# Values and inverse products of each recurrent group tied to a counted number of other blocks' products; the visits of the state chain joined, on two banks

## The chip, the cores and the metric

The kernel runs on one core of one Trainium2 chip. The metric is the device time of one execution in microseconds (us), from the first to the last instruction and what little lies around them. Engines are named as in the profile: PE is the matmul engine (PEld its weight loads), DVE the vector engine, ACT the scalar engine, POOL the third elementwise engine, SP the engine from whose queue all DMAs are issued.

## The reference

One layer of a hybrid decoder on 1024 tokens of 1024 channels: three branches on the same normalised input, merged by gates, then a ConvFFN. Cut to what matters here:

```python
h = rms_norm(x, norm_mix_pre)
z = h @ w_in                                   # one input projection for all branches
z_pool, z_q, z_rwkv, z_gate = split(z)
y_pool = pool_branch(z_pool) @ w_proj_pool     # causal means over windows 2, 4, 8, 16
y_mem = mem_attention(z_q, mem_n) @ w_proj_mem # 4 heads into 256 memory tokens
r, k, v, dw, da, dg = split(zr)                # zr: z_rwkv mixed with its token shift
# recurrent branch, 16 heads of 64, for every token t:
sa = state @ a_t
state = state * w_t + sa b_t^T + v_t k_t^T
y_t = state @ r_t
# then a norm per head, + bonus: sum(r * k * r_k) * v, times a gate g
merged = g0 * y_pool + g1 * (y_rwkv @ w_proj_rwkv) + g2 * y_mem
x = x + rms_norm(merged @ w_o)
f = (gelu(u_gate) * u_val) @ w_ffn_down        # u: causal conv of rms_norm(x) @ w_ffn_up
x = x + rms_norm(f)
```

## The kernel before

**Products in three parts.** Activations lie transposed (channels on partitions, tokens along the row). A large product is made of three passes on values split into a high and a low part: `mm3` (L158) issues high x high (L161), high weights x low activations (L162) and low weights x high activations (L163). The input projection is cut into 58 blocks of 128 output channels. A block (`in_block`, L249) loads eight 128x128 weight pieces, two per DMA (`load_w`, L139: raw on SP's queue, high part on POOL or ACT, low part on POOL or DVE), and makes two halves of 512 tokens, each of eight steps; a step is the three products of one weight piece. So a block has 16 steps or 48 products. `hh` and `hl` hold the split input.

**Groups.** The 16 recurrent heads are done in four groups of two head pairs (`rwkv_group`, L376). A group has these stages:

- the vector stage (L390 to L446): decay and rate from their small projections, head sums (`phd`), scans, scaled copies `AR` and `BK` for each head pair, and the block of r (L421, in_block). At the end of each pair's part stands the bonus: a product of ones `pbo` (L442) that must stand behind the scaling of r (L439), its product with v on DVE (L443), ACT, and a store to `d_bv`, which is read back only at the group's end (L599).
- the values (`pv`, L458 and L459): v centred, into `HV`.
- the scores (`ps`, L479 and L486): products within chunks of 64 tokens, masked on DVE into `RB`, `NT` and `AR`; then BK scaled (L491) and transposed (`pt`, L496).
- the inverse: 32x32 triangles of both pairs inverted on DVE by substitution (L513 to L518), transposed (L519, L520), then completed by small products `pz` (L534) and `pw` (L541). All `pz` products stand behind L520.
- the state chain (L549 to L590): 16 rounds, one per chunk. In a round PE makes `pr`, DVE copies it to `Rs`, PE makes `pu`, DVE and ACT copy it into `HV`, PE makes `ph` (the new state) and `py` (the output, partly L564, partly L586), and DVE adds `ph` into the next state. `pr`, `pu` and `ph` use one bank (`psc`), one after another.
- the four blocks of k and v of the next group (`group_kv`, L354), then the head norm of this group's output (L595 to L613).

**What sets the order.** The framework lays down the order on each engine when the program is built. It takes the program's order as priority and places an instruction as soon as its own estimates say that its inputs are there; what is ready and stands later in the program goes into the gaps. Tiles of one tag take their buffers in program order. `later` (L199) adds an order between two instructions without a wait. 24 of the 32 blocks of the pooling input, the queries and the gates (`fill`, L616) stand behind the four groups in the program and have weight buffers and banks of their own (class 1), so that they can be drawn into the gaps of the groups. The last eight stand in the pooling stage (two per pool group, L739).

**After the groups** come the memory's keys and values (L643), the attention (L679), the pooling stage (L718), the projections of the memory branch (L763) and of the pooling branch (L773) and the rest. The tiles `pm` of the memory projection lie where `hh` and `hl` were. `load_w` without a class alternates between class 0 and class 1.

## Time and profile before

| | |
|---|---|
| median of 3 runs | 2258.53 us (2258.16 to 2258.91) |
| the profiled execution | 2256.94 us, of which span 2255.2 us |
| mean granted PE clock | 0.982 of full speed |
| groups 0 to 3 | about 114 to 1035 us of the span |
| PE, DVE, ACT, POOL busy | 96%, 52%, 37%, 34% of the span |

Times of single instructions are us from the start of the span. Where an engine waited, the views name what released it last. "PE pz L534 <- DVE tb L519" reads: the product into pz issued in line 534 stood until DVE's instruction on tb in line 519 was done. A row of a table by stretches gives the stretch, its length, then for each engine the busy time and, in brackets, the number of instructions, then the granted PE clock, the share of time in which DMA engines were busy, and GB/s.

### The profile page before, as it was taken

To read this page: it belongs to the slowest core of one execution; us is meant where nothing else is said; L and a number is where in the kernel's file an instruction comes from. 1 tells how busy PE (TensorE), PEld (TensorE's weight loads), DVE (VectorE), ACT (ScalarE), POOL (GpSimd) and SP (SyncE) were. 2 spreads that over 40 slices of the span, in tenths; PEclk is the share of its full clock that TensorE was granted. 3 is DMA by queue.
4 is the path that set the end of the run, shared out by engine and by line. 5 is a ranking of instruction groups with operands and counts; after the bars stand their busy time and mean duration, and the time that the engine had idled before them with its cause. 6 is when DMAs were issued, how large, how long until landed. Compare 5 with 4: busy or idle time off the path is not lost.

```text
span 2255.2 us, 34230 instructions
## 1 busy us (share of the span) xinstructions
PE 2155.7 (96%) x12630; PEld 1649.1 (73%) x12630; DVE 1176.7 (52%) x2101; ACT 837.1 (37%) x1696; POOL 766.4 (34%) x1025
## 2 busy tenths in 40 slices
PE   7999899989998999899989999999999999999998
PEld 4767566766676667667877878777888888888887
DVE  6277539653965386634764442767403423334237
ACT  3342234223432252224634244545433413323143
POOL 6552116222521242212153355556422222323240
PEclk9999999999998999999999999999999999999999
DMA  4311112112111121114336343543211111111123
GB/s 138 126 54 50 38 60 68 57 39 67 66 55 41 54 92 44 57 56 142 98 117 201 130 145 100 163 153 94 76 50 45 50 50 42 54 40 57 38 75 136
DMA packets 147319, 181.46 MB, mean 80 GB/s; under 512 B 15824, under 2 KB 115792, under 8 KB 147152
## 3 DMA queue, kind: packets, MB, share of 16 engines
q1 hardware_dynamic: 147152, 179.28, 24.4%
q8 instruction: 100, 1.64, 0.3%
q14 instruction: 67, 0.55, 0.1%
HBM read 141.46 MB, written 37.75 MB: 79 GB/s over the span
## 4 chain that ended last, share of the span: by engine, by line
PE 73%; DVE 17%; DMA 3%; ACT 3%; issue 2%; POOL 2%; SPq 0%; POOLq 0%; ACTq 0%; DVEq 0%
PE psg L161 20%; PE psg L162 20%; PE psg L163 20%; DVE tb L518 2%; DVE tb L516 2%; PE ps L486 2%; PE ps L479 1%; POOL wlo L127 1%; PE pr L554 1%; PE pu L560 1%; ACT tHV L191 1%; DVE AR L425 1%; PE py L564 1%; PE py L586 1%; DMA wraw<-in_w_in 1%
## 5 line engine op out<-in xcount | busy, mean ns | idle before, releaser
L127 POOL TENSOR_TENSOR wlo<-wraw,whi 128x256 fp32r<-128x256 f32 (+1 forms) x696 | 578.3, 835 | 686.7 <-ACT whi L124 606.3
L161 PE MATMUL psg<-hh,whi 128*128 128x512 f32 x928 | 389.2, 420 | 0.9 <-ACT hh L117 0.7
L162 PE MATMUL psg<-hl,whi 128*128 128x512 f32 x928 | 386.6, 417 | 1.6 <-DVE hl L118 1.6
L126 POOL TENSOR_SCALAR whi<-wraw 128x256 fp32r<-128x256 f32 x240 | 151.3, 630 | 695.4 <-PE psg L162 671.9
L163 PE MATMUL psg<-hh,wlo 128*128 128x512 f32 x928 | 384.1, 414 | 0.2
L124 ACT CAST whi<-wraw 128x256 fp32r<-128x256 f32 (+1 forms) x488 | 191.8, 401 | 361.5 <-PE psg L162 274.2
L161 PE MATMUL psg<-h2h,whi 128*128 128x512 f32 x704 | 279.7, 397 | 4.4 <-DVE zc L826 4.4
L163 PE MATMUL psg<-h2h,wlo 128*128 128x512 f32 x704 | 278.7, 396 | 1.2 <-POOL wlo L127 1.2
L162 PE MATMUL psg<-h2l,whi 128*128 128x512 f32 x704 | 278.6, 396 | 0.0
L161 PEld LDWEIGHTS psg<-hh,whi 128*128 128x128 f32 x928 | 177.0, 191 | 47.0 <-issue 2.2
L163 PEld LDWEIGHTS psg<-hh,wlo 128*128 128x128 f32 x928 | 177.4, 191 | 43.2 <-issue 2.2
L162 PEld LDWEIGHTS psg<-hl,whi 128*128 128x128 f32 x928 | 177.0, 191 | 43.0 <-DVE hl L118 2.5
L161 PEld LDWEIGHTS psg<-h2h,whi 128*128 128x128 f32 x704 | 132.4, 188 | 37.3 <-ACT whi L124 5.0
L163 PEld LDWEIGHTS psg<-h2h,wlo 128*128 128x128 f32 x704 | 132.3, 188 | 34.2 <-POOL wlo L127 1.6
L162 PEld LDWEIGHTS psg<-h2l,whi 128*128 128x128 f32 x704 | 132.4, 188 | 32.7 <-issue 0.5
L823 DVE SCALAR_TENSOR_TENSOR uv<-psg,pv,uv 128x511 f32<-128x511 f32 x44 | 33.0, 749 | 156.7 <-ACT uv L822 156.7
L163 PE MATMUL psg<-fh,wlo 128*128 128x512 f32 x288 | 113.8, 395 | 0.0
L162 PE MATMUL psg<-fl,whi 128*128 128x512 f32 x288 | 113.8, 395 | 0.0
L161 PE MATMUL psg<-fh,whi 128*128 128x512 f32 x288 | 113.6, 395 | 0.0
L823 DVE SCALAR_TENSOR_TENSOR ug<-psg,pv,ug 128x511 f32<-128x511 f32 x44 | 32.9, 749 | 146.2 <-ACT ug L822 146.2
L989 DVE TENSOR_TENSOR acc<-acc,psg 128x512 f32<-128x512 f32 x48 | 33.0, 687 | 102.5 <-PE psg L163 102.5
L276 ACT ACTIVATE st<-psg,pv 128x512 f32<-128x512 f32 x48 | 33.1, 690 | 108.9 <-PE psg L163 99.1
(341 smaller groups left out, 3975.0 us busy)
## 6 DMA issues: line engine op xcount, KB each, us to landing
wraw<-in_w_in SPq DMA_DIRECT2D x240, 128.0 KB, 2.3
wraw<-in_w_fup SPq DMA_DIRECT2D x216, 128.0 KB, 2.3
d_zg<-st SPq DMA_DIRECT2D x48, 256.0 KB, 2.6
wraw<-in_w_fdn SPq DMA_DIRECT2D x80, 128.0 KB, 2.1
wraw<-in_w_prwkv SPq DMA_DIRECT2D x64, 128.0 KB, 2.3
wraw<-in_w_o SPq DMA_DIRECT2D x64, 128.0 KB, 2.3
xr<-in_xT SPq DMA_DIRECT2D x16, 256.0 KB, 5.4
d_g<-st SPq DMA_DIRECT2D x16, 256.0 KB, 2.0
```

The costliest lines, as they stand in the source:

```text
L124: A.copy(hi, src)
L126: G.tensor_scalar(hi, src, 1.0, 0.0, op0=ALU.mult, op1=ALU.add)
L127: (V if lo_on_dve[0] else G).tensor_tensor(lo, src, hi.bitcast(F32), op=ALU.subtract)
L161: first = PE.matmul(ps, wh, xh, start=start, stop=False)
L162: PE.matmul(ps, wh, xl, start=False, stop=False)
L163: last_mm[0] = PE.matmul(ps, wl, xh, start=False, stop=stop).ins
L276: A.activation(st, ps, AF.Identity, bias=bias)
L486: PE.matmul(ps[:, c], BK[i][up, c0 + c], AR[up, i, 1:3, t], start=True, stop=True)
L516: V.tensor_tensor(tm, X[:, s + 1:, s:s + 1].broadcast_to([P, n, m]), S[:, s:s + 1, 0:m].broadcast_to([P, n, m]), op=ALU.mult)
L518: V.tensor_tensor(S[:, s + 1:, 0:m], S[:, s + 1:, 0:m], tm, op=ALU.add)
L823: V.scalar_tensor_tensor(d[:, 1:], ps[:, :511], col("cw1", j), d[:, 1:], op0=ALU.mult, op1=ALU.add)
L989: V.tensor_tensor(accs[n][:, j], accs[n][:, j], ps, op=ALU.add)
```

## The change

Four things are changed.

1. The 24 blocks are no longer behind the groups in the program. `fill_to(n)` issues whole blocks until at least n steps of them stand in the program, and returns the last product of step n. In group g the first value product is ordered behind step 95 g + 28, and the first inverse product `pz` behind step 95 g + 95 (380 of 384 in the last group). The order of every `pz` behind L520 is dropped.
2. The bonus of both head pairs is made behind the scores of the first pair, and no longer ordered behind the scaling of r.
3. In the state chain `pr`, `pu` and `ph` take turns on two banks (`psc` and `psk`).
4. The chain's products form three visits per round: `pr` with the first part of `py`; `pu`; `ph` with the second part of `py`. Within a visit each product is ordered behind the one before, and the first behind the last copy or sum that it needs.

The eight blocks of the pooling stage stay the same ones.

```diff
@@ gemm
+            if log is not None:
+                log.append(last_mm[0])
@@ rwkv_group, vector stage
             V.scalar_tensor_tensor(t0_, r_, col("r_k", p), t4_, op0=ALU.mult, op1=ALU.mult)
-            rt = V.tensor_tensor(r_, r_, t3_, op=ALU.mult).ins
+            V.tensor_tensor(r_, r_, t3_, op=ALU.mult)
+            vs.append(t1_)
+
+        def bonus(i):
+
+            t0_ = kv[i][:, 0]
             for t0, _ in HALVES:
+                s = slice(t0, t0 + 512)
                 ps = pss.tile([P, 512], F32, name="pbo", tag="s")
-                later(PE.matmul(ps, bones, t0_[:, t0:t0 + 512], start=True, stop=True), rt)
-                V.tensor_tensor(t0_[:, t0:t0 + 512], t1_[:, t0:t0 + 512], ps, op=ALU.mult)
-            A.activation(t0_, t0_, AF.Identity, bias=col("ln_b", p))
-            SP.dma_start(d_bv[p], t0_)
-            vs.append(t1_)
+                PE.matmul(ps, bones, t0_[:, s], start=True, stop=True)
+                V.tensor_tensor(t0_[:, s], vs[i][:, s], ps, op=ALU.mult)
+            A.activation(t0_, t0_, AF.Identity, bias=col("ln_b", 2 * g + i))
+            SP.dma_start(d_bv[2 * g + i], t0_)
...
+        place = fill_to(95 * g + 28)
...
-                    PE.matmul(ps[64:128, c], vs[i][0:64, tsl], cent[0:64], start=True, stop=True)
+                    m = PE.matmul(ps[64:128, c], vs[i][0:64, tsl], cent[0:64], start=True, stop=True)
+                    if i == c0 == c == 0:
+                        later(m, place)
...
+            for b in range(2 if i == 0 else 0):
+                bonus(b)
...
-        behind = V.transpose(X.rearrange("p u t -> p t u"), S).ins
+        V.transpose(X.rearrange("p u t -> p t u"), S)
+        place = fill_to(95 * g + 95)
...
-                    later(m, behind)
+                    if u0 == u == 0:
+                        later(m, place)
@@ state chain
+        turn = [0]
+
+        def bank(name):
+            turn[0] ^= 1
+            return (psc if turn[0] else psk).tile([P, 2, C], F32, name=name, tag="c" if turn[0] else "k")
+
+        def visit(products, after):
+
+            for (out_, l, r), kw in products:
+                m = PE.matmul(out_, l, r, **kw)
+                if after is not None:
+                    later(m, after)
+                after = m.ins
+            return after
+
+        ready = None
         for c in range(NCH):
             t = slice(c * C, (c + 1) * C)
-            pr = psc.tile([P, 2, C], F32, name="pr", tag="c")
+            once = dict(start=True, stop=True)
+            pr = bank("pr")
+            py = pss.tile([P, 2, C], F32, name="py", tag="s")
+            ke, ko = (up, lo) if c == 0 else (slice(0, P), slice(0, P))
+            row = []
             for i in range(2):
-                ke, ko = (up, lo) if c == 0 else (slice(0, P), slice(0, P))
-                PE.matmul(pr[lo, i], AR[ke, i, 0, t], HV[ke, i, c, 0], start=True, stop=True)
-                PE.matmul(pr[up, i], AR[ko, i, 2, t], HV[ko, i, c, 1], start=True, stop=True)
+                row.append(((pr[up, i], AR[ko, i, 2, t], HV[ko, i, c, 1]), once))
+                row.append(((pr[lo, i], AR[ke, i, 0, t], HV[ke, i, c, 0]), once))
+            for i in range(2 if c else 0):
+                kw = dict(start=i == 0, stop=False)
+                row.append(((py[lo, i], HV[lo, i, c, 0], AR[lo, i, 1, t]), kw))
+                row.append(((py[up, i], HV[up, i, c, 1], AR[up, i, 1, t]), kw))
+            visit(row, ready)
             Rs = rw.tile([P, 2, C], F32, name="Rs", tag="Rs", bufs=1)
             V.tensor_copy(Rs, pr)
-            pu = psc.tile([P, 2, C], F32, name="pu", tag="c")
+            pu = bank("pu")
+            visit([((pu[q, i], NT[q, i, c], Rs[q, i]), once) for i in range(2) for q in (lo, up)], None)
+            V.tensor_copy(HV[lo, :, c, 0], pu[lo])
+            ready = A.copy(HV[up, :, c, 1], pu[up]).ins
+            row = []
+            if c + 1 < NCH:
+                ph = bank("ph")
+                for i in range(2):
+                    row.append(((ph[up, i], BKN[i][:, c, 64:128], HV[:, i, c, 1]), once))
+                    row.append(((ph[lo, i], BKN[i][:, c, 0:64], HV[:, i, c, 0]), once))
             for i in range(2):
...
+                kw = dict(start=c == 0 and i == 0, stop=i == 1)
+                row.append(((py[lo, i], HV[:, i, c, 0], RB[i][:, 0, c]), kw))
+                row.append(((py[up, i], HV[:, i, c, 1], RB[i][:, 1, c]), kw))
+            visit(row, ready)
             if c + 1 < NCH:
...
                 for q, e in ((lo, 0), (up, 1)):
                     if c == 0:
-                        V.tensor_copy(HV[q, :, 1, e], ph[q])
+                        ready = V.tensor_copy(HV[q, :, 1, e], ph[q]).ins
                     else:
-                        V.tensor_tensor(HV[q, :, c + 1, e], ph[q], Hd[q], op=ALU.add)
+                        ready = V.tensor_tensor(HV[q, :, c + 1, e], ph[q], Hd[q], op=ALU.add).ins
...
@@ trunk_kernel
+    filled = []
+
+    def fill_to(n):
+
+        while len(filled) < n:
+            j, ev = fill.pop(0)
+            in_block(j, ev, 1, filled)
+        return filled[n - 1]
+
...
-    for j, ev in fill[:24]:
-        in_block(j, ev, 1)
...
-            n = 16 + 2 * gi
-            for j, ev in gates[n:n + 2]:
+            for j, ev in fill[2 * gi:2 * gi + 2]:
                 in_block(j, ev, 1)
```

More of the change, by code (lines that the diff above doesn't have):

```diff
@@ L164, in mm3, with gemm @@
         return first
-    def gemm(ws, rhs, width=512, behind=None, ps=None):
+    def gemm(ws, rhs, width=512, behind=None, ps=None, log=None):
         if ps is None:
@@ L247, in hrhs, with in_block @@
         return lambda k: (hh[:, k, t0:t0 + 512], hl[:, k, t0:t0 + 512])
-    def in_block(j, evac, c=0):
+    def in_block(j, evac, c=0, log=None):
         ws = load_w(w_in[j], KC, c=c)
         for t0, _ in HALVES:
-            evac(t0, gemm(ws, hrhs(t0)))
+            evac(t0, gemm(ws, hrhs(t0), log=log))
     def shifted(m, dst):
@@ L556, in rwkv_group @@
             Rs = rw.tile([P, 2, C], F32, name="Rs", tag="Rs", bufs=1)
             V.tensor_copy(Rs, pr)
-            pu = psc.tile([P, 2, C], F32, name="pu", tag="c")
-            for i in range(2):
-                PE.matmul(pu[lo, i], NT[lo, i, c], Rs[lo, i], start=True, stop=True)
-                PE.matmul(pu[up, i], NT[up, i, c], Rs[up, i], start=True, stop=True)
-            py = pss.tile([P, 2, C], F32, name="py", tag="s")
-            for i in range(2 if c else 0):
-                PE.matmul(py[lo, i], HV[lo, i, c, 0], AR[lo, i, 1, t], start=i == 0, stop=False)
-                PE.matmul(py[up, i], HV[up, i, c, 1], AR[up, i, 1, t], start=i == 0, stop=False)
@@ L566, in rwkv_group @@
-            V.tensor_copy(HV[lo, :, c, 0], pu[lo])
-            A.copy(HV[up, :, c, 1], pu[up])
+            pu = bank("pu")
[8 more added lines that the diff above has]
+                    row.append(((ph[lo, i], BKN[i][:, c, 0:64], HV[:, i, c, 0]), once))
@@ L568, in rwkv_group @@
+            for i in range(2):
+                kw = dict(start=c == 0 and i == 0, stop=i == 1)
+                row.append(((py[lo, i], HV[:, i, c, 0], RB[i][:, 0, c]), kw))
+                row.append(((py[up, i], HV[:, i, c, 1], RB[i][:, 1, c]), kw))
+            visit(row, ready)
             if c + 1 < NCH:
-                ph = psc.tile([P, 2, C], F32, name="ph", tag="c")
-                for i in range(2):
-                    PE.matmul(ph[lo, i], BKN[i][:, c, 0:64], HV[:, i, c, 0], start=True, stop=True)
-                    PE.matmul(ph[up, i], BKN[i][:, c, 64:128], HV[:, i, c, 1], start=True, stop=True)
@@ L584, in rwkv_group @@
                         A.activation(Hd[:, i], Hn[:, i], AF.Identity, scale=Dc[:, i, c + 1:c + 2])
-            for i in range(2):
-                PE.matmul(py[lo, i], HV[:, i, c, 0], RB[i][:, 0, c], start=c == 0 and i == 0,
-                          stop=i == 1)
-                PE.matmul(py[up, i], HV[:, i, c, 1], RB[i][:, 1, c], start=c == 0 and i == 0,
-                          stop=i == 1)
             A.copy(AR[:, :, 1, t], py)
@@ L714, in trunk_kernel @@
     as_ctx.close()
-    gates = fill[8:]
     with tc.tile_pool(name="pt", bufs=1) as pt_:
```

## The prediction, made before the result was known

> **What bounds the kernel now.** I read the page first, then who waited for whom on the matmul engine within the four recurrent groups (110 to 1040 us), then the granted clock right behind the longest wait.
>
> ```profile
> span 2255.2 us, 34230 instructions
> PE 2155.7 (96%) x12630; PEld 1649.1 (73%) x12630; DVE 1176.7 (52%) x2101; ACT 837.1 (37%) x1696; POOL 766.4 (34%) x1025
> ...
> PE pz L534 <- DVE tb L519: 30.3, 4, 7.7
> PE pbo L442 <- DVE kv L438: 12.6, 8, 3.5
> ...
> PE phd L372 <- DVE kv L443: 1.1, 4, 0.4
> PE pv L458 <- DVE kv L443: 0.8, 3, 0.3
> ```
>
> PE is busy for 96% of the span: it is the bound, and only three things can shorten the kernel: less PE idle time, less PE time at a low clock, less PE time per product. The waits (total, times, longest) name two places. Once per group PE stands about 7.6 us before the first inverse product (pz, L534) until DVE has finished the inverse (L519), and twice per group it stands before the bonus product (pbo, L442). With the two small followers these are 30.3 + 12.6 + 1.1 + 0.8 = 44.8 us.
>
> The clock comes next. The columns are stretch, length, busy time (instructions) of PE, PEld, DVE, ACT and POOL, granted clock, DMA share and GB/s; then three products of the first stretch.
>
> ```profile
> 241.00:248.30 7.30, 7.30 (x77) 5.26 (x77) 4.00 (x6) 3.65 (x7) 2.20 (x4) 0.50 0.06 20
> 469.96:476.90 6.94, 6.94 (x77) 5.27 (x77) 5.55 (x10) 4.31 (x7) 1.90 (x3) 0.50 0.06 19
> 697.84:704.80 6.96, 6.96 (x77) 5.27 (x77) 4.53 (x8) 4.88 (x8) 0.00 (x0) 0.50 0.01 2
> 928.82:935.00 6.18, 6.18 (x76) 4.83 (x77) 3.98 (x6) 3.13 (x6) 0.00 (x0) 0.54 0.01 3
> 209.00:233.50 24.50, 24.50 (x106) 19.36 (x104) 22.44 (x50) 3.00 (x6) 10.76 (x18) 1.00 0.26 86
> ...
> 850.90:854.80 3.90, 3.88 (x68) 2.62 (x68) 2.59 (x3) 1.13 (x1) 0.23 (x1) 1.00 0.11 35
> ...
> 246.10 0.63 PE L161 MATMUL psg<-hh,whi 128*128 128x512 f32 x1
> 246.53 0.63 PE L162 MATMUL psg<-hl,whi 128*128 128x512 f32 x1
> ```
>
> Behind each of the four waits PE runs some 7 us at half clock: its wide products start 0.43 us apart (246.10 to 246.53), against 24.50 / 106 = 0.231 us in the dense stretch before. So each wait costs more than its own length.
>
> **The change, part by part.** I count in steps of three wide products, 0.69 us each. The rows are the products on hh (columns: stretch, length, busy time and count, clock, DMA share, GB/s); two of a step's three use hh, so steps are the count halved. The page's count of L161 gives 928 steps in all.
>
> ```profile
> L161 PE MATMUL psg<-hh,whi 128*128 128x512 f32 x928 | 389.2, 420 | 0.9 <-ACT hh L117 0.7
> ...
> 0.00:928.80 928.80, 505.44 (x1451) 0.97 0.20 66
> 114.00:163.30 49.30, 34.77 (x108) 1.00 0.14 46
> 163.30:240.90 77.60, 37.24 (x111) 0.98 0.17 58
> 928.80:1141.00 212.20, 99.41 (x252) 0.98 0.26 87
> 1141.00:1212.00 71.00, 50.56 (x153) 0.95 0.39 132
> ```
>
> *Values and inverse behind counted steps.* In group 0 now 54 steps lie before the values and 55.5 between them and the inverse. Afterwards it is the group's 32 steps of r plus 28, that is 60, and then 95 - 28 = 67: 6 and 11.5 more, 17.5 x 0.69 = 12.1 us of work that is due anyway. It goes where PE now stands 44.8 / 4 = 11.2 us. So both waits should close and the group's first two stages keep their length; the counts overshoot by about 1 us, which is work, not loss. **Term 1: -44.8 us.** What is then late at the inverse is the count itself, not DVE.
>
> *Half clock.* Without a 7 us gap the products behind it run at full clock. Half of 27.4 us (the four stretches) is the upper bound, 13.7. The lower bound is the eleven wide products in each stretch, at 0.43 - 0.23 = 0.20 us: 8.8. I take **term 2: -11 us**. [...]
>
> *Bonus moved* behind the first head pair's scores. Its DVE work stays:
>
> ```profile
> L443 DVE TENSOR_TENSOR kv<-kv,pbo 128x512 f32<-128x512 f32 x4 | 2.5, 674 | 0.0
> ```
>
> Four of 0.67 us leave the vector stage and enter the score stage, before the BK scaling and the inverse. Earlier start and later work cancel: 0. If the earlier start isn't had, 2.7 us per group, 10.8 in all, delay the inverse. The bonus stores go to SP's queue later, but are read back only at the group's end (L599), so nothing waits.
>
> *The chain's visits.* A visit is a run of small products between wide ones. Rows of one round, then the one place where two visits already touch:
>
> ```profile
> 264.88 0.27 PE L554 MATMUL pr<-HV,AR 128*64 128x64 f32 x1
> ...
> 265.26 0.50 PE L162 MATMUL psg<-hl,whi 128*128 128x512 f32 x1
> ...
> 267.43 0.27 PE L586 MATMUL py<-RB,HV 128*64 128x64 f32 x1
> ...
> 268.09 0.50 PE L162 MATMUL psg<-hl,whi 128*128 128x512 f32 x1
> ...
> 268.75 0.27 PE L564 MATMUL py<-AR,HV 64*64 64x64 f32 x1
> ...
> 269.15 0.50 PE L161 MATMUL psg<-hh,whi 128*128 128x512 f32 x1
> 269.58 0.27 PE L554 MATMUL pr<-HV,AR 128*64 128x64 f32 x1
> ...
> 278.84 0.27 PE L565 MATMUL py<-AR,HV 64*64 64x64 f32 x1
> ...
> 279.10 0.27 PE L554 MATMUL pr<-HV,AR 128*64 128x64 f32 x1
> ...
> 279.48 0.33 PE L565 MATMUL py<-AR,HV 64*64 64x64 f32 x2
> ```
>
> A round lasts 269.58 - 264.88 = 4.70 us and has four visits; the py visit (L564) is now put with pr (L554). Apart the two cost 0.40 (268.75 to 269.15) + 0.43 for the wide product between, less its own 0.23, + 0.38 (264.88 to 265.26) = 0.98 us. Touching they cost 0.40 + 0.38 = 0.78, since pr takes 0.38 behind py too (279.10 to 279.48). So 0.20 us each, 15 rounds x 4 groups: **term 3: -12.0 us**. Sixteen products of one form take only 0.66 (267.43 to 268.09); at that price it would be 0.32 x 60 = 19. [...]
>
> The second bank costs nothing: psk's bank is otherwise used from L646 on. It spares pr the wait for the Hn sum, which is no bound now. The new order chains py behind the last copy; I price that as a rival.
>
> *What is taken from later.* By 928.8 us 725.5 steps are done now. With the change 26 blocks x 16 + 380 = 796 are done at that place (the fourth inverse), and 132 are left. The stages up to 1141 now take 126 as fill, so about 6 remain for the pooling stage, which now has 76.5.
>
> ```profile
> 1141.00:1212.00 71.00, 65.42 (x262) 50.08 (x261) 41.50 (x55) 21.39 (x36) 40.71 (x45) 0.95 0.39 132
> ...
> 1141.35 0.33 SPq L723 DMA_DIRECT2D tz<-d_zp  x1
> ...
> 1154.30 0.38 SPq L723 DMA_DIRECT2D tz<-d_zp  x1
> ...
> 1170.65 1.33 SPq L723 DMA_DIRECT2D tz<-d_zp  x1
> ...
> 1186.90 0.33 SPq L723 DMA_DIRECT2D tz<-d_zp  x1
> ...
> 1209.32 0.42 SPq L768 DMA_DIRECT2D pm<-d_zg  x1
> ...
> L161 PE MATMUL psg<-oh,whi x64: 392/395/398, 1209.8 to 1254.7; 128*128 128x512 f32 x64
> ```
>
> That stage has a chain of its own, one load and one pass of DVE per pool group, 13 to 16 us each: 1141.35 to 1186.90, and one more of about 16, makes some 63 us however little PE does. Now PE has 262 x 0.232 = 61 us of products there, in 71: 10 lost. What can fill it is the memory projection (192 products, oh), which starts at 1209.8, when the last block on hh is done and its memory free (pm at 1209.32). With that done by about 1145 its first products can come forward; but it alternates two weight and bank classes, and the second class shares its banks with the pool products, so I let half through: 96. Work then is 18 + 24 (pool) + 96 = 138 x 0.232 = 32 us in 63: 31 lost, 21 more than now. **Term 4: +21 us.** Ends: none comes forward, +43; all, about 0.
>
> Sum on the profiled execution's own time: 2256.9 - 44.8 - 11 - 12 + 21 = 2210.1. The median of the runs is 1.6 us above that execution, so **2212 us**.
>
> **The rivals.**
> *Nothing fills the pool stage*: the projection stays behind the pool products. For: it starts after the last block now. Price: 96 x 0.232 = 22 us; 2234.
> *All of it fills*: both classes come forward, 22 us less; 2190. For: pm waits for the last hh block alone in the rows.
> *The closed-up visits wait.* Now L564 stands right behind DVE:
>
> ```profile
> 268.75 0.13 PEld L564 LDWEIGHTS py<-AR,HV 64*64 64x64 f32 x1 [0.36 <-DVE HV L577]
> ```
>
> If one wide product too few is laid into the two gaps behind the copies, each round waits up to 2 x 0.23, 64 rounds 29 us; 2241. Against: the four gaps of a round hold nine wide products, and three gaps with fewer copies between need fewer.
> *Slower: the counted products come on top of the waits.* Place: 6 steps before the values, 11.5 before the inverse. If they only delay the scores, the inverse starts later by as much and PE stands as before: +12.1 x 4 = 48.4, terms 1 and 2 gone. Then only the visits (12) and the shorter late stages are left: pooling and projection last 1255 - 1141 = 114 us now and 63 + 22 = 85 then, 29 less. 2258.5 + 48.4 - 12 - 29 = 2266. It decides from 41 of the 48 us on top. Against: the wait ends with DVE, and steps laid before it are used up while DVE works.
> *Nothing happens*, because the order hardly moves: 2258.
>
> **How the numbers follow.** Forecast 2212: 0.45. Pool stage empty, 2234: 0.20. Full, 2190: 0.14. Visits wait, 2241: 0.08. On top, 2266: 0.08. No effect: 0.05. Under 0.2% (4.5 us) this kernel can't be told from no change. Faster 0.87, same 0.05, slower 0.08. The range 2187 to 2240 takes the first three cases with the bounds of terms 2 and 4.
>
> **What would show it.** Right: no wait of pz on L519 above 1 us, clock 1.00 behind each inverse, no pbo wait, three visits per round, about 796 steps done at the fourth inverse, PE idle and at low clock between the pool groups, oh products before the last pool product. Wrong: pz still waiting (counts too small, or on top), new waits of pr, pu or ph inside the chain, or an attention stage that has run out of fill.

## The result and the profile after

| | before | after |
|---|---|---|
| median of 4 runs each | 2258.61 us (2258.16 to 2258.91) | 2272.68 us (2272.32 to 2273.62) |
| the profiled execution | 2256.9 us, span 2255.2 | 2272.8 us, span 2271.1 |
| mean granted PE clock | 0.982 | 0.964 |

The ratio is 1.0063, with a 95% interval of 1.0046 to 1.0081. The kernel became 0.6% slower, where the forecast was 2% faster. The range of the forecast, 2187 to 2240 us, missed it.

The page of the changed kernel, the rows that answer to those shown of before:

```profile
span 2271.1 us, 34255 instructions
...
PE 2174.0 (96%) x12630; PEld 1665.0 (73%) x12630; DVE 1182.3 (52%) x2101; ACT 839.3 (37%) x1696; POOL 748.6 (33%) x1025
```

PE does the same 12630 products and is busy 18 us longer. Who waited for whom on PE (total, times, longest):

```profile
PE pz L547 <- DVE tb L531: 20.6, 4, 5.2
...
PE pw L555 <- ACT tb L550: 7.1, 4, 1.8
PE psg L163 <- POOL wlo L127: 6.7, 8, 0.9
```

The waits for the bonus are gone. The wait at the inverse's first products (pz) is still there, 5.2 us a group where it was 7.7, and a new one of 1.8 us stands at its second products (pw). Filling steps now also wait for the low parts of their weights (6.7 us in all), which none did in the groups before. Next the clock right behind these waits: stretch, length, busy time and number of instructions of PE, PEld, DVE, ACT and POOL, clock, DMA share, GB/s. The first five rows follow group 0 without a break, the last three are the other groups.

```profile
248.80:255.00 6.20, 4.43 (x77) 3.49 (x78) 4.34 (x7) 3.62 (x6) 0.00 (x0) 0.50 0.10 36
255.00:262.00 7.00, 7.00 (x136) 5.08 (x135) 0.70 (x1) 1.73 (x3) 0.00 (x0) 0.50 0.03 10
262.00:270.00 8.00, 8.00 (x78) 5.00 (x77) 0.00 (x0) 1.15 (x2) 0.00 (x0) 0.50 0.01 2
270.00:275.20 5.20, 5.20 (x40) 3.42 (x38) 1.35 (x5) 1.11 (x4) 0.00 (x0) 0.53 0.00 0
275.20:282.00 6.80, 6.80 (x83) 4.57 (x78) 2.99 (x10) 2.22 (x7) 1.54 (x3) 1.00 0.07 20
492.40:517.00 24.60, 22.75 (x310) 15.89 (x311) 5.78 (x11) 6.95 (x13) 0.00 (x0) 0.50 0.04 13
736.50:761.00 24.50, 22.62 (x310) 15.75 (x310) 5.68 (x11) 6.86 (x12) 0.00 (x0) 0.50 0.04 12
974.90:1002.00 27.10, 25.28 (x328) 17.45 (x328) 6.42 (x13) 7.71 (x15) 0.00 (x0) 0.50 0.03 11
```

Here time was lost. Before, PE ran some 7 us at half clock behind each inverse, 27.4 us in all. Now it runs about 25 us: busy 4.43 + 7.00 + 8.00 + 5.20 + 22.75 + 22.62 + 25.28 = 95.3 us at half clock. If half of each is lost, that is 47.6 us against 13.7, so 34 us more. This is an estimate, and rather a high one: 64 small pz products take 1.92 us at half clock and 1.20 at full (rows of exact28 and exact28_wide below). PE's busy time bears it out: it is 18 us longer, although the new visits alone (chain_only below) make it 14.5 us shorter. In the second and third row PE doesn't stand for a moment in 15 us, and the clock still doesn't come back.

What PE did at the start of that stretch, from its timeline (start, duration, line, product, count, idle time before it):

```profile
248.86 1.92 PE L547 MATMUL pz<-tb,NT 32*32 32x32 f32 x64 [4.93 <-DVE tb L531]
250.71 0.69 PE L572 MATMUL pr<-HV,AR 64*64 64x64 f32 x8
251.33 0.79 PE L161 MATMUL psg<-hh,whi 128*128 128x512 f32 x1
251.92 0.63 PE L162 MATMUL psg<-hl,whi 128*128 128x512 f32 x1
254.26 0.31 PE L555 MATMUL pw<-NT,tb 32*32 32x32 f32 x2 [1.71 <-ACT tb L550]
```

Behind the products that had waited come two wide products, a new wait, and then (to 262 us) three wide ones, pw, pz, and single wide ones between pu. Before, eleven wide products stood in the first 7 us.

The late stages did what was forecast. Products on hh (two of a step's three) up to the fourth inverse and from there to the pooling stage, the first load of the pooling stage, and the memory projection's products:

```profile
0.00:974.90 974.90, 560.48 (x1600) 0.95 0.20 68
974.90:1185.80 210.90, 89.59 (x231) 0.93 0.25 84
```

```profile
1186.11 0.33 SPq L763 DMA_DIRECT2D tz<-d_zp  x1
```

```profile
L161 PE MATMUL psg<-oh,whi x64: 387/395/628, 1195.2 to 1274.0; 128*128 128x512 f32 x64
```

1600 / 2 = 800 steps are done at the fourth inverse (796 were forecast). The pooling stage begins at 1186.1 instead of 1141.3, 44.8 us late, and the span ends 15.9 us late. So the late stages are 28.9 us shorter. Not all of the 44.8 us is a loss: by then 1831 / 2 = 915.5 steps are done instead of 851.5, and these 64 steps at 0.69 us are 44 us of work moved forward. So up to the pooling stage the change gained next to nothing, where the forecast had 67.8 us (terms 1 to 3). The 15.9 us by which the kernel is longer are about what the late stages lose for want of filling work, which the forecast had put at 21. The oh products start before the pooling stage is over, as the forecast had it.

### The profile page after: what moved, and what is told of

Same layout as the page of the kernel before. It is cut to its first block, busy times and chain, and to the rows that moved or that the text cites. A ratio compares the mean times of both kernels' runs of the same rounds, so it can differ in the third digit from the quotient of the medians.

```text
span 2271.1 us, 34255 instructions
## 1 busy us (share of the span) xinstructions
PE 2174.0 (96%) x12630; PEld 1665.0 (73%) x12630; DVE 1182.3 (52%) x2101; ACT 839.3 (37%) x1696; POOL 748.6 (33%) x1025
## 4 chain that ended last, share of the span: by engine, by line
PE 79%; DVE 10%; DMA 3%; issue 3%; POOL 2%; ACT 2%; SPq 0%; POOLq 0%; ACTq 0%; DVEq 0%
PE psg L161 22%; PE psg L163 22%; PE psg L162 21%; DVE tb L528 3%; DVE tb L530 2%; PE py L572 2%; POOL wlo L127 2%; PE ps L496 1%; PE ps L489 1%; PE pu L572 1%; PE pr L572 1%; PE ph L572 1%; PE pw L555 1%; POOL whi L126 1%; PE pv L466 1%
## 5 line engine op out<-in xcount | busy, mean ns | idle before, releaser
L127 POOL TENSOR_TENSOR wlo<-wraw,whi 128x256 fp32r<-128x256 f32 (+1 forms) x696 | 573.6, 828 | 671.8 <-ACT whi L124 612.9
L126 POOL TENSOR_SCALAR whi<-wraw 128x256 fp32r<-128x256 f32 x240 | 135.3, 564 | 729.3 <-PE psg L162 669.9
```

The lines of the kernel that those rows point to most:

```text
L126: G.tensor_scalar(hi, src, 1.0, 0.0, op0=ALU.mult, op1=ALU.add)
L127: (V if lo_on_dve[0] else G).tensor_tensor(lo, src, hi.bitcast(F32), op=ALU.subtract)
```

## The experiments

Every kernel computes the whole layer. The runs were made on several chips, each beside runs of the kernel before, so the table goes by ratios to before.

| kernel | median us | ratio | 95% interval |
|---|---|---|---|
| the changed kernel | 2272.68 | 1.0063 | 1.0046 to 1.0081 |
| chain_only | 2238.58 | 0.9923 | 0.9906 to 0.9939 |
| bonus_back | 2267.08 | 1.0054 | 1.0039 to 1.0069 |
| values18 | 2256.42 | 1.0009 | 1.0000 to 1.0019 |
| inv103 | 2258.96 | 1.0018 | 1.0008 to 1.0027 |
| exact28 | 2251.86 | 1.0002 | 0.9984 to 1.0021 |
| exact18 | 2262.31 | 1.0033 | 1.0022 to 1.0044 |
| nohold | 2273.84 | 1.0077 | 1.0056 to 1.0098 |
| wide_behind | 2234.65 | 0.9913 | 0.9892 to 0.9933 |
| narrow_behind | 2249.03 | 0.9975 | 0.9965 to 0.9985 |
| sparse_behind | 2278.24 | 1.0106 | 1.0086 to 1.0126 |
| exact28_wide | 2217.79 | 0.9835 | 0.9821 to 0.9850 |
| wide26 | 2221.38 | 0.9854 | 0.9819 to 0.9888 |
| wide24 | 2249.69 | 0.9978 | 0.9960 to 0.9995 |
| wide32 | 2260.78 | 1.0003 | 0.9977 to 1.0030 |
| split24 | 2227.63 | 0.9868 | 0.9848 to 0.9889 |

**The parts by themselves.** The expectations call PE TensorE, DVE VectorE and ACT ScalarE. The first question was which part brings the long half clock: the counted places (theory 1), the closed-up visits (theory 2), or the moved bonus (theory 3). chain_only is the kernel before with the new state chain alone:

```diff
--- before
+++ chain_only
+        def bank(name):
...
+        def visit(products, after):
...
-            pr = psc.tile([P, 2, C], F32, name="pr", tag="c")
+            pr = bank("pr")
+            py = pss.tile([P, 2, C], F32, name="py", tag="s")
...
+            visit(row, ready)
```

> The kernel before with the closed-up visits and the two banks alone. Theory 1 (the counts stand in the wrong places for the real DVE): the visits do their 12 us, 2246 us, three visits per round, and the half-clock stretch behind each inverse stays near the 7 us of before. Theory 2 (the closed-up chain itself makes the stretch long, because fewer wide products lie between its visits): half clock for some 25 us behind each inverse as in the changed kernel, four times 18 us at half worth 9 us each, so 2258 - 12 + 36 = 2282 us.

It took 2238.58 us, 0.77% less than before. Its wait at the inverse and two of the four stretches behind it:

```profile
PE pz L534 <- DVE tb L519: 30.8, 4, 8.1
```

```profile
240.80:248.30 7.50, 7.49 (x83) 5.39 (x85) 3.99 (x6) 3.82 (x7) 2.34 (x4) 0.51 0.06 20
462.90:470.00 7.10, 7.10 (x77) 5.25 (x77) 3.96 (x6) 3.04 (x5) 0.00 (x0) 0.50 0.01 2
```

The wait is as long as before, and the stretch at half clock too: 7 us. So theory 2 falls: the closed-up chain does not bring the long stretch. Three starts of a round's first visit (pr), from its timeline:

```profile
263.40 0.45 PE L558 MATMUL pr<-HV,AR 128*64 128x64 f32 x8
...
268.12 0.45 PE L558 MATMUL pr<-HV,AR 128*64 128x64 f32 x8
...
272.13 0.45 PE L558 MATMUL pr<-HV,AR 128*64 128x64 f32 x8
```

The second round lasts 4.01 us and holds seven wide products; a round of before lasted 4.70 and held nine. Without the wide ones at 0.232 us that is 2.39 against 2.61: 0.22 us saved a round, the forecast's 0.20.

bonus_back is the changed kernel with the bonus in its old place:

```diff
--- after
+++ bonus_back
-        def bonus(i):
...
+                later(PE.matmul(ps, bones, t0_[:, t0:t0 + 512], start=True, stop=True), rt)
+                V.tensor_tensor(t0_[:, t0:t0 + 512], t1_[:, t0:t0 + 512], ps, op=ALU.mult)
...
-            for b in range(2 if i == 0 else 0):
-                bonus(b)
```

> The changed kernel with the bonus back at the end of each pair's vector part. Theory 1: DVE's 5.6 us of standing between the scores of the two pairs goes, the inverse is ready about 5 us earlier, so pz's wait of 5 us is nearly gone and the half clock with it: 2205 to 2225 us. Theory 3 alone (only the bonus matters, the clock follows something else): 4 x 5 = 20 us, 2252 us. If the waits for pbo come back (12.6 us) with no gain at pz: 2275 us or more.

1.0054 against 1.0063: the intervals lie over each other. PE waits 11.0 us for the bonus again and 4.1 us less at the inverse (16.5 instead of 20.6). Moving the bonus is worth nothing that these runs can tell, and theory 3 falls. The run missed theory 1's time as well, and all three of its cases. It shows that the bonus waits could be closed without a gain: what goes at pbo comes back as 4.1 us at the inverse and 4.7 us at the weights of filling steps (2.0 us there in bonus_back, 6.7 in the changed kernel).

**The counts.** values18 asks for 18 steps before the values instead of 28, inv103 for 103 steps a group.

```diff
--- after
+++ values18
-        place = fill_to(95 * g + 28)
+        place = fill_to(95 * g + 18)
```

> The changed kernel with the values behind step 18 of the group in place of step 28. Theory 1: the scores start 6 us earlier (DVE stood 12 us before them in group 0), the inverse is done before step 95, PE's wait at pz (20.6 us in four) and at pw (7.1) is gone, and with it the half clock (25 us per group, worth 12): about 2272 - 28 - 48 = 2196 us, up to 2215 if the pooling stage runs emptier. Theory 3 (the bonus in the score stage is the delay, the values' place is not): the scores start no earlier relative to the end of the vector stage, less than 8 us gained, 2265 us or more.

```diff
--- after
+++ inv103
-        place = fill_to(95 * g + 28)
+        place = fill_to(103 * g + 28)
...
-        place = fill_to(95 * g + 95)
+        place = fill_to(103 * g + 103)
```

> The changed kernel with 103 steps per group in place of 95 before the inverse (values still 28 into the group): 5.5 us more work before pz. Theory 1: pz no longer waits, full clock behind it: 2272 - 28 - 48 = 2196 us, less 22 us that 32 steps fewer leave to fill in the pooling stage, so 2196 to 2220 us. Theory 2: the half clock comes with the closed-up chain: the waits go (28 us), the half clock stays, 2245 us or more.

Both gained about 0.5% on the changed kernel, far from the 2196 us and more of theory 1, and both only in two of four groups: values18 in groups 2 and 3, inv103 in 0 and 2. Windows of inv103 behind its four inverses:

```profile
261.00:268.00 7.00, 7.00 (x214) 5.21 (x213) 1.51 (x3) 2.89 (x5) 1.13 (x2) 1.00 0.25 86
493.00:518.00 25.00, 23.05 (x311) 15.96 (x311) 6.16 (x12) 7.13 (x13) 0.00 (x0) 0.51 0.03 12
749.00:756.00 7.00, 7.00 (x214) 5.32 (x213) 1.69 (x3) 2.99 (x5) 1.01 (x2) 1.00 0.24 80
975.50:1002.00 26.50, 24.66 (x327) 17.01 (x327) 6.38 (x13) 7.71 (x15) 0.00 (x0) 0.50 0.03 12
```

The reason for the pattern is in the code. `fill_to` issues whole blocks of 16 steps into the program, and what stands earlier in the program goes first. A count of 28 is met by 32 steps, one of 95 by 96; in values18 the counts 18 and 113 still round to 32 and 128, and only 208 and 303 round to other blocks (208 and 304) than in the changed kernel (224 and 320). The blocks laid between the values and the inverse then hold 64, 64, 80 and 80 steps in values18, 80, 64, 80 and 64 in inv103, and 64 in every group of the changed kernel: the groups with 80 are those that gained. In values18 they pay for it: between one inverse and the next values 16 steps are left in place of 32 ahead of groups 2 and 3, and there the values wait 6.0 and 4.7 us for ACT. So in the changed kernel the values stand behind 4 to 7 steps more than was asked, and DVE, which needs them for the scores, stands meanwhile. From DVE's timeline in group 0, first before, then after:

```profile
164.89 1.27 DVE L443 TENSOR_TENSOR kv<-kv,pbo 128x512 f32<-128x512 f32 x2
172.49 0.42 DVE L480 TENSOR_TENSOR RB<-ps,mincl 128x256 f32<-128x256 f32 x1 [6.33 <-PE ps L479]
```

```profile
159.84 1.63 DVE L441 TENSOR_TENSOR AR<-AR,tBN 128x1024 f32<-128x1024 f32 x1
173.48 0.42 DVE L490 TENSOR_TENSOR RB<-ps,mincl 128x256 f32<-128x256 f32 x1 [12.02 <-PE ps L489]
```

DVE is done 4.7 us earlier (161.5 instead of 166.2), then stands 12.0 us instead of 6.3. The four bonus instructions (2.7 us) come on top in the score stage, and at the inverse DVE is again what PE waits for. Of the 7.9 us by which the inverse's products start later in group 0 (248.9 against 241.0), 1.0 is there at the first scores, 4.5 come on in the score stage, and 2.4 in the inverse itself.

To take the rounding away, the next kernels issue the filling steps one by one:

```diff
--- after
+++ exact28
+    def in_steps():
+        while True:
+            j, ev = fill.pop(0)
...
+                for k in range(KC):
+                    mm3(ps, ws[k], x(k), k == 0, k == KC - 1)
+                    filled.append(last_mm[0])
...
+                    yield
...
-            j, ev = fill.pop(0)
-            in_block(j, ev, 1, filled)
+            next(stepper)
```

> The changed kernel, but the filling products are issued step by step, so that a count of 28 (values) and 95 (inverse) behind 95 per group is met exactly and not at the end of a whole block of 16 steps (32 and 96). Theory 1 (the counts land late by the rest of the block, VectorE stands meanwhile, and what it lost comes back as the 5.2 us wait in front of the inverse's products and as the half clock behind it): the values begin 4 steps sooner, about 4 x 1.1 = 4.4 us, the inverse one step sooner; the wait at the inverse falls from 5.2 us to about 2 us a group, and the time to 2240 to 2262 us. Theory 2 (the closed-up groups lose by something that the place of the values does not touch): 2268 to 2278 us, wait 4 to 6 us a group.

exact18 is the same with a count of 18, nohold the same with the values behind no step at all:

```diff
--- exact28
+++ exact18
-        place = fill_to(95 * g + 28)
+        place = fill_to(95 * g + 18)
--- exact28
+++ nohold
-        place = fill_to(95 * g + 28)
...
-                    if i == c0 == c == 0:
-                        later(m, place)
```

> The same with the values behind exactly 18 steps (the inverse behind 95). Theory 1: all four groups go as the groups 2 and 3 of the run with a count of 18 in whole blocks did (74 to 89 us from the inverse's first product to the first variance against 101 us): no wait above 1 us at the inverse, clock 1.00 behind it, four times some 13 us less than the changed kernel, about 2220 us (2205 to 2240); if the values come before ScalarE has their inputs, a wait of up to 5 us stands in front of them, and 2240 us. Theory 2: 2260 us or more.

> The same with the values not held behind any step; the inverse alone stands behind exactly 95. Theory 1: the values start as soon as their inputs are there, VectorE never stands, no wait at the inverse and clock 1.00 behind it: 2205 to 2240 us, within 10 us of the run with exactly 18. Theory 3 (values that are not held take TensorE in the vector stage or wait for ScalarE in front of ready steps): waits of 5 to 10 us a group at the values, 2240 to 2265 us.

exact28 met its forecast: waits at pz of 6.0 instead of 20.6 us, 1.0002. But its runs spread from 2250 to 2266 us, its waits at pw grew to 11.7 us, and in its profiled execution, one of the longer ones, the half clock had not gone. exact18 and nohold fell out against theory 1. They have no wait at the inverse, and the values now wait for ACT (ScalarE in the expectations; 19.0 and 20.3 us in four groups), with the half clock behind them. Windows of exact18:

```profile
162.40:189.50 27.10, 27.10 (x106) 19.85 (x103) 11.10 (x25) 1.83 (x4) 0.00 (x0) 0.50 0.00 1
408.40:411.20 2.80, 2.74 (x52) 2.74 (x54) 0.39 (x1) 1.88 (x5) 0.00 (x0) 0.50 0.40 140
411.20:420.00 8.80, 8.80 (x66) 6.62 (x63) 5.00 (x13) 1.61 (x3) 0.00 (x0) 0.99 0.00 0
```

In group 0 the clock stays at 0.50 for 27 us behind a wait of 3.4 us; in group 1 it is back after 2.8 us of products, behind a longer wait (5.8 us). Those products are all small ones, 64x64 products of the values, without a wide one among them. What follows, the scores in eights with one or two wide products between, is the same in both groups; it keeps half clock in the one and full clock in the other. So the length of a wait does not set the length of the stretch, and neither does the inverse. That left the question of what does.

**What stands behind the wait.** wide_behind puts six whole steps between the inverse's two product groups:

```diff
--- after, with the steps of exact28
+++ wide_behind
-        place = fill_to(95 * g + 28)
+        place = fill_to(96 * g + 32)
...
-        place = fill_to(95 * g + 95)
+        place = fill_to(96 * g + 90)
...
+            if u0 == 0:
+                place = fill_to(96 * g + 96)
...
+                    m = PE.matmul(ps[q0, u], Z[q1, u0 + u], NTu[q1, u0 + u, 32:64], start=True, stop=True)
+                    if u0 == u == 0:
+                        later(m, place)
```

> The changed kernel with whole steps of filling work between the inverse's two product groups: values behind 32, the first product group of the inverse behind 90, the second behind 96, so that six steps (18 wide products, some 6 us) stand right behind the first products that waited. Theory A (the half clock lasts 25 us in the changed kernel because hardly a wide product follows the wait, 2 to 4 at a time between small products): the wait grows to 9 to 11 us a group, but the stretch at clock 0.50 falls to 7 to 10 us, so the time is 2245 to 2265 us. Theory B (the length of the stretch goes by the wait, or by what else the group does): the stretch stays at 24 us or more, and the time is 2285 to 2300 us.

0.9913: below the range that theory A gave, and far from theory B. The wait at the inverse had grown to 7.4 us a group, as long as before the change, and yet the kernel is 1.5% faster than the changed one. Its clock in group 0:

```profile
248.40:252.90 4.50, 4.47 (x70) 3.95 (x71) 3.35 (x5) 2.73 (x5) 0.03 (x1) 0.50 0.02 4
252.90:262.00 9.10, 9.10 (x224) 7.03 (x223) 1.69 (x3) 2.62 (x5) 3.40 (x6) 1.00 0.23 75
```

narrow_behind took the order of pw behind the six steps back and was meant as the other side of the comparison.

> wide_behind with one edit taken back: the second product group of the inverse isn't held behind six steps, so that small products follow the waiting ones at once, as in the changed kernel; values behind exactly 32, inverse behind exactly 90 stay. Theory A (a long stretch at clock 0.50 comes where few wide products follow a wait): the wait at the inverse stays at about 7 us a group as in wide_behind, the stretch behind it goes from 7 to 10 us back to 24 us or more, and the time to 2265 to 2285 us. Theory B (wide_behind was faster because the inverse begins after 90 exact steps, not by what stands behind it): 2230 to 2245 us.

It missed: 0.9975, the stretch 5 to 7 us, the time between the two theories. The order explains the stretch: the framework had by itself laid ten wide products from later in the program between pz and pw, so the edit did not take the wide products away. (Of the 14 us to wide_behind, 8 are waits of the small projections for POOL, psu on ulo: 9.2 us against 1.1.) sparse_behind does take them away:

```diff
--- narrow_behind
+++ sparse_behind
+    held = []
...
         first = PE.matmul(ps, wh, xh, start=start, stop=False)
+        if held:
+            later(first, held.pop())
...
+            if u0 == 0:
+                held[:] = [m.ins] * 160
```

> narrow_behind with all further wide products of the group held behind the inverse's second product group, so that none stands between the two groups (ten did); the same work, moved by some 2 to 10 us. Theory A: the wait at the inverse stays about 7.4 us a group, one of 1 to 3 us at the second group comes on top, and the stretch at 0.50 goes from 7 to 10 us to 20 us or more in every group: 2249 + 4 x (2 + 7 to 10) = 2285 to 2300 us. Theory B: only the new wait is paid, 2253 to 2262 us, stretch below 12 us.

exact28_wide does the opposite to exact28, and nothing else:

```diff
--- exact28
+++ exact28_wide
+            if u0 == 0:
+                place = fill_to(95 * g + 101)
...
+                    if u0 == u == 0:
+                        later(m, place)
```

> exact28 (values behind 28, inverse behind 95) with one edit: the second product group of the inverse stands behind step 101, so six steps of wide products lie between the two. [...] Theory B (what stands behind the wait is of no account): 2245 us or more.

Both came out as theory A had it (few wide products behind a wait make the stretch long), but for sparse_behind's time, 7 us below its range. exact28_wide, forecast at 2212 to 2232 us with no wait left at pw, took 2217.79 us and has no such wait among the named ones. Taking the wide products away costs 1.3% (0.9975 to 1.0106), putting them in gains 1.7% (1.0002 to 0.9835). Not all of that is the clock: packed products between pz and pw also fill the wait at pw, 10.8 us in sparse_behind and 11.7 in exact28. Some 19 and 26 us are left. Windows behind the inverse, narrow_behind's group 0, then sparse_behind's four groups:

```profile
247.90:252.50 4.60, 4.60 (x77) 4.03 (x78) 3.60 (x6) 2.88 (x5) 0.00 (x0) 0.50 0.02 4
252.50:262.00 9.50, 9.50 (x215) 6.85 (x215) 1.39 (x2) 2.52 (x6) 0.00 (x0) 1.00 0.01 2
```

```profile
248.20:276.90 28.70, 25.89 (x339) 18.08 (x341) 6.84 (x14) 7.29 (x15) 0.00 (x0) 0.50 0.01 2
...
497.30:520.00 22.70, 19.94 (x305) 14.47 (x306) 5.68 (x11) 6.32 (x12) 0.00 (x0) 0.51 0.01 2
744.30:768.00 23.70, 20.95 (x306) 14.85 (x306) 6.20 (x12) 6.86 (x14) 0.00 (x0) 0.50 0.01 2
988.40:1012.00 23.60, 20.81 (x314) 14.93 (x314) 6.24 (x12) 6.57 (x13) 2.62 (x5) 0.52 0.04 13
```

And exact28 against exact28_wide in group 0, one window behind the inverse each, then the rows of pz:

```profile
246.40:272.50 26.10, 24.35 (x321) 16.69 (x323) 6.12 (x12) 7.62 (x15) 0.00 (x0) 0.50 0.09 27
```

```profile
249.00:255.40 6.40, 4.77 (x11) 3.80 (x12) 2.00 (x5) 3.84 (x7) 0.34 (x1) 0.51 0.33 102
255.40:262.00 6.60, 6.60 (x176) 4.94 (x176) 0.99 (x2) 1.73 (x3) 0.80 (x2) 0.96 0.19 63
```

```profile
246.36 1.92 PE L547 MATMUL pz<-tb,NT 32*32 32x32 f32 x64 [2.88 <-DVE tb L531]
```

```profile
246.90 1.20 PE L547 MATMUL pz<-tb,NT 32*32 32x32 f32 x64 [2.88 <-DVE tb L531]
```

The wait before pz is 2.88 us in both. In exact28 it is followed by half clock for 26 us; in exact28_wide pz runs at full clock, half clock comes at 249 with a later stop of 1.63 us, and the clock is back 6.4 us on, behind eleven packed wide products. Where wide products were packed behind pz at half clock, full clock came 4.5 us (wide_behind) and 4.6 us (narrow_behind) behind its start; in exact18's group 1, behind small products, after 2.8 us. PE's busy share alone does not tell when it comes: between 255 and 270 us the changed kernel's PE is busy for 15.0 of 15.0 us, and keeps 0.50. What the clock goes by, no run here shows.

**Towards a better place.** Four kernels looked for counts at which nobody waits, with the wide products behind the inverse. First the three that differ from wide_behind only in numbers (before the values, before pz, before pw: 26, 96, 101 and 24, 98, 103 with 95 a group; 32, 104, 109 with 96):

```diff
--- wide_behind
+++ wide26
-        place = fill_to(96 * g + 32)
+        place = fill_to(95 * g + 26)
...
-        place = fill_to(96 * g + 90)
+        place = fill_to(95 * g + 96)
...
-                place = fill_to(96 * g + 96)
+                place = fill_to(95 * g + 101)
```

> wide_behind with the values behind 95g+26, the first product group of the inverse behind 95g+96 and the second behind 95g+101: the vector engine stands less ahead of the scores, so the wait at the inverse should go with no more steps. Theory A: wait at the inverse at most 2 us a group, clock 0.50 for 7 us a group or less, 2200 to 2220 us. Theory C: 2225 to 2238 us. If the values now wait for ScalarE, 1 to 3 us a group stand in front of them, with half clock behind, and 2215 to 2240 us.

> The same with 95g+24, 95g+98 and 95g+103. Theory A: no wait at the inverse; with a wait at the values of 1 to 4 us a group (5 us at a count of 18), 2205 to 2230 us; if the wait at the values brings long half clock there (few wide products follow the values before the scores), 2225 to 2250 us.

> wide_behind with more steps ahead of the inverse: values behind 96g+32, first product group behind 96g+104, second behind 96g+109, so that 14 more steps lie where the matmul engine stood 7.4 us. Theory A: the wait at the inverse goes (below 1 us a group), clock 0.50 lasts 7 us a group or less, and the time falls by most of the 29 us of waits, to 2205 to 2222 us. Theory C (steps used here are missing from the pooling stage, whose own chain sets its length): waits gone, but late stages longer by as much, 2225 to 2238 us.

wide26 came out where its third case (values that wait for ScalarE, ACT in the profile) had it (0.9854), wide24 lay at the upper end of its worst case (0.9978), and wide32 missed all of its cases (1.0003; its runs spread from 2238 to 2265 us, and the profiled one is the longest). All three have no wait at the inverse left among the named ones. They differ in what the values wait for ACT: 5.2 us in two groups, 10.5 in three, 15.6 in three. What was overlooked is that the counts run on from group to group: more steps ahead of one inverse leave fewer between it and the next group's values. That distance is 96 + 32 - 104 = 24 in wide32, 95 + 24 - 98 = 21 in wide24, 25 in wide26, 18 in exact18 (19.0 us of waits), 28 in exact28_wide (2.5 us) and 38 in wide_behind (none). From the values to the inverse it is 58 steps in wide_behind (29.4 us of waits at pz), 64 in the changed kernel (20.6), 67 in exact28 (6.0) and 70 in wide26 (none). The waits do not follow the distance strictly (24 steps wait longer than 21), but some 70 and some 30 seem to be wanted, 100 a group, and all of these kernels have 95 or 96: one of the two always comes short. A count of 100 a group was not tried step by step; inv103 has 103, rounded to whole blocks.

split24 put the values in two halves, behind 24 and 29, with the second products of the inverse behind 102:

```diff
--- wide26
+++ split24
-        place = fill_to(95 * g + 26)
+        place = fill_to(95 * g + 24)
...
+            if i == 1:
+                place = fill_to(95 * g + 29)
```

> wide26 with the values in two halves, the first behind 95g+24 and the second behind 95g+29, and the second product group of the inverse behind 95g+102: wide products stand where the values waited for ScalarE (5.2 us in two groups of wide26). If those waits go and no other comes: 2205 to 2218 us, no stretch at half clock in front of the scores. If ScalarE is late whatever stands there (its queue holds the stores of the filling blocks): waits move to the steps, 2218 to 2240 us.

0.9868: no gain on wide26. The values wait as long (5.0 us against 5.2), the steps wait for the stores' ACT work (5.0 us), which speaks for ACT's queue being late and not the place of the second half.

exact28_wide and wide26 both beat the kernel before and the changed one, by 1.6% and 1.5% of before; the runs do not tell them apart. About half of that is the visits: chain_only, with nothing else changed, has 0.8%.

## Why the prediction was wrong

The predicted span to the pooling stage was 47 - 29 = 18 us shorter than before; it is 44.8 us longer. The miss of 63 us lies ahead of the pooling stage, and most of it is there at the fourth inverse (974.9 us instead of 928.8). By the prediction's own steps:

- **Term 2, the half clock (-11): the step that failed most.** It came to some +34 us (the estimate above), a miss of 45. The prediction took 7 us at half clock as what a wait brings, and asked only whether the wait goes. It counted the eleven wide products that stand in each stretch, as the lower bound of a price, and did not see that the length of the stretch hangs on them. The change moves wide products from behind the inverse to before it, and two were left between pz and pw. sparse_behind (28.7 us in group 0 where narrow_behind had 4.6) and exact28_wide (6.4 us where exact28 had 26.1) show this from both sides.
- **The length of a wait does not tell whether the clock goes.** In the kernel before, the clock was 1.00 behind the 3.5 us wait for pbo (850.90). Behind a wait of 2.88 us exact28 had 26 us of half clock, though exact28_wide's pz kept full clock behind the same wait; there half clock came with the later stop of 1.63 us. So "without a 7 us gap the products behind it run at full clock" was the author's estimate, and it did not hold: no wait at pz in the changed kernel is longer than 5.2 us, and half clock stands behind all four.
- **Term 1, the waits (-44.8): half right.** The steps came nearly as counted (in group 0 64 before the values and 64.5 behind them, where 60 and 67 were meant) and the waits for the bonus went, but pz and pw still wait 20.6 + 7.1 = 27.7 us. "What is then late at the inverse is the count itself, not DVE" was wrong: the values feed DVE, and holding them holds DVE. "The group's first two stages keep their length" fell with it. Part of it is the rounding to whole blocks, which was in the diff and was overlooked: exact28 brings the wait at pz to 6.0 us.
- **Bonus moved (0): right as a sum**, by bonus_back. The earlier start (4.7 us in group 0) was lost at the values, as in the case that the prediction priced at 10.8 us; but the old place costs as much in waits.
- **Term 3, the visits (-12): right in mechanism and nearly in size.** 0.22 us a round where 0.20 was forecast; chain_only as a whole gained 0.77%, that is 17 us (14 to 21). What the rest of some 4 us is was not looked for.
- **Term 4, the late stages: right, in mechanism too.** 29 us shorter forecast, 28.9 measured; by 1250 us half of the memory projection's products had run (65 of the 128 on oh), and half was what the forecast let through.

45 and 27.7 less the 4 to 5 us that the visits gave more make some 68 us. The miss is 63, and 6.5 steps fewer than forecast were moved forward (64 instead of 70.5), which is 4.5 us: the two sides agree as far as the estimate of the half clock goes.

Of the rivals the slower one was nearest, 2266 us, with a chance of 0.08. Its sign was right and its sum near, its mechanism right in part: the inverse does start later (7.9 us in group 0) and PE does still stand before it. But its price was the whole count on top of the wait, while a good half of what terms 1 and 2 missed is the clock; that the sum came near is in part luck. What the prediction said against it, that "steps laid before it are used up while DVE works", holds for steps before the inverse and not for those before the values. No visit waits inside the chain (0.3 us for pr in all), so that rival fell.

## What to carry to other kernels

Before closing a wait on the matmul engine with work from elsewhere, look at what that work was doing where it stood: in these runs a stop of 2.9 to 7.7 us could cost its own length plus 3 to 29 us at half clock, and the length of that stretch went by whether several us of packed products followed at once (wide ones, or in one case 2.8 us of small ones). Where a stop can't be avoided, keep such a pack for the place right behind it (six steps here, worth 1.7% with the wait that they fill). And a count that holds back a product holds back every engine that this product feeds (here DVE stood 12.0 us before the first scores, 6.3 before the change), so count from each hold to the next, round the whole loop.

## What the hardware showed

**Half clock without a pause.** PE kept half clock for 23 to 29 us while it stood for 1.8 to 2.8 us of them, as long as small products and single wide ones took turns (sparse_behind and the changed kernel), and was back at 1.00 after 4.5 us where wide ones were packed (wide_behind). Such a mix didn't take the clock away either: in exact18 it kept 0.99 from 411 to 420 us in group 1, and in inv103 the inverses without a wait kept 1.00. In these rows the mix keeps the clock that it met.

**DVE beside POOL's splits.** In the changed kernel DVE's two lines of the inverse's substitution take 61.2 + 52.9 us instead of 51.1 + 52.7. Rows of POOL and of DVE at the same time:

```profile
217.68 0.74 POOL L127 TENSOR_TENSOR wlo<-wraw,whi 128x256 fp32r<-128x256 f32 x1
```

```profile
217.73 0.82 DVE L528 TENSOR_TENSOR tb<-tb 128x112 f32<-128x112 f32 x1
218.59 0.28 DVE L530 TENSOR_TENSOR tb<-tb,tb 128x112 f32<-128x112 f32 x1
```

Of two DVE instructions on 112 elements the one that begins under POOL's split of a weight takes 0.82 us and ends 0.13 us behind POOL's (218.55 against 218.42), the next takes 0.28. Over all 248 instructions of these two lines, each measured by the shortest of its form in the two kernels, those that no split runs beside lose 0.4 us in all, before as after. Those beside a split's low part (L127) are 64 before and lose 18.4 us, 96 after and lose 28.9. So by these rows filling steps cost DVE time too, through the splits of their weights: 10.5 us more over the four groups here, on the chain that ends before pz. No run took the splits away.
